# A two-layer diffusion backbone on one core: the third FFN's first product as seven block products for 18 of its 22 pairs, and an earlier place for DeltaNet's gate sums

## Chip, core and metric

The kernel runs on one core of a Trainium2 chip. The metric is the device time of one launch in microseconds (us). Engines are named as the profile names them: PE is TensorE, with PEld its weight loads; DVE is VectorE, ACT ScalarE, POOL GpSimd; SP issues most DMAs. The engines run unsynchronized; each works through its own list of instructions in order and waits on semaphores.

## What is computed

Two layers over 512 tokens, 256 of context and 256 latent, of width 1024. Each layer is a feed-forward network (FFN), a token mixer (DeltaNet in layer 0, windowed attention in layer 1) and a second FFN, each behind a modulated RMS norm. So there are four FFNs; the third, first of layer 1, is the one that the change rewrites. Its mathematics is

```python
def _swiglu(h, w1, w2):
    a, b = jnp.split(h @ w1, 2, axis=-1)
    return (jax.nn.silu(a) * b) @ w2
```

with h 512 x 1024, w1 1024 x 5632 and w2 2816 x 1024, all float32. The modulation vectors (shift, scale, gate) come from the conditioning times a matrix `ada_w` of 1024 x 9216 per layer. DeltaNet's part that the change touches is the running sum of its log gates g over chunks of 64 tokens.

## The kernel before, in words

**Layout.** Activations stand transposed: a tile has 128 channels on the partitions and 512 tokens along the free axis, context in columns 0 to 255 (`CTX`), latent in 256 to 511 (`LAT`). `self.X` is the residual stream (8 tiles), `self.H` the normed input of a product (8 tiles), `self.G` the FFN's gated hidden.

**Products in split form.** A float32 operand is split in two reduced-precision parts (fp32r), `hi` and `lo`, with lo = x - hi; a product is three matmuls: hi·hi, hi·lo, lo·hi (`mm3`, L292). So one 128-wide block of outputs over all 512 tokens and 1024 input channels takes 8 x 3 = 24 matmuls of 128 rows, 128 columns and 512 moving columns.

**An FFN.** The 22 pairs (128 columns of a and the matching 128 of b) go in three parts of 6, 8 and 8 (`self.parts`). For a part, `ffn1_pairs` (L1000) makes each pair with 48 matmuls, in a PSUM tile for a and one for b. `ffn_evac` (L872) is the evacuation: silu(a) on ACT, times b on DVE, copy to `hi` on ACT, subtraction to `lo` on DVE. Then `out_blocks` (L1057) multiplies the part by w2: 8 output tiles, each 3 matmuls for every pair of the part. In the first part of an FFN the first two pairs run the context half first and then the latent half (`halves_first`, L1018), since the normed input arrives by halves and tile by tile (`h_chunks`, L818, fed by ACT, DVE and POOL).

**Weights.** `plan_weights` (L306) lists loads of 1 MB (`raw`, two buffers, and `ub`, two more) and units, the weight blocks in the order of their use. `_split` (L447) makes a unit's `hi` by a copy on ACT and its `lo` by a subtraction on DVE. `w_ahead` (L483) is a background task that keeps up to `LOOK` = 4 units split ahead of the one in use.

**Background work.** `ada_gen` (L682) makes the modulation vectors: for each, 16 steps load a 128x512 piece of `ada_w` and multiply by the conditioning and accumulate, on DVE alone or with the product on ACT and the addition on POOL. In the third FFN it runs until 1371 us.

**What sets the order.** The program's text is written by generators under a planning clock (`Sched`, L69): every matmul advances the clock, and a task runs when the clock reaches the time at which it expects its input (`at`, L249). `spare` (L253) is `at` with 2500 ns more. The clock decides only the place of an instruction in its engine's list; on the chip, semaphores decide the time. The clock holds a cost for each engine's instruction and knows of no interference between engines.

**DeltaNet's gates.** `dn_gates` (L1202) takes the product's gate columns, transposes them on PE, applies softplus and scaling on ACT and DVE, and writes `gs`. Then five small matmuls on `gs` make the sums; from them DVE makes `glb`, `kdl`, `neg` and ACT makes `eg`, `aS`. Around it, `dn_unit` (L1262) takes the keys' tiles through a 5-tap convolution on DVE (four SCALAR_TENSOR_TENSOR after an ACT copy, for each head), silu on ACT, and four transposes on PE.

Of the kernel before, what the change touches and what calls it, by code (L numbers as in the profile page):

```python
# [213 lines left out]
class Kernel:  # L214
# [57 lines left out]
    def mm(self, out, lhsT, rhs, start=True, stop=True, tp=None, ns=None):  # L272
        kw = {} if tp is None else {"tile_position": tp}
# [10 lines left out]
        self.nc.tensor.matmul(out, lhsT, rhs, start=start, stop=stop, **kw)  # L284
        self.s.tick(ns)
# [6 lines left out]
    def mm3(self, ps, w, h, nk, sl=ALL, ks=None, start=True, stop=True):  # L292

        whi, wlo = w
        hhi, hlo = h
        ks = range(nk) if ks is None else ks
        for i, k in enumerate(ks):
            if h is self.H:
                self.h_wait(k, sl)
            wh, wl = whi[k // 4][:, k % 4, :], wlo[k // 4][:, k % 4, :]  # L300
            self.mm(ps[:, sl], wh, hhi[k][:, sl], start=(start and i == 0), stop=False)
            self.mm(ps[:, sl], wh, hlo[k][:, sl], start=False, stop=False)
            self.mm(ps[:, sl], wl, hhi[k][:, sl], start=False, stop=(stop and i == len(ks) - 1))


    def plan_weights(self):  # L306
# [13 lines left out]
        def unit(r, views, shape):  # L320
            for i in r:
                self.raws[i]["left"] += 1
            self.units.append({"r": r, "views": views, "shape": shape, "w": None})

        def cols(mat, r0, nk, c0, w=256):

# [6 lines left out]
        def ffn1(w1, p0, n):  # L333
            if n % 2:
                r = raw((lambda t: t[:, :, 0:128], w1[:, 128 * p0:128 * p0 + 128].rearrange("(k p) c -> p k c", p=128)),
                        (lambda t: t[:, :, 128:256],
                         w1[:, F + 128 * p0:F + 128 * p0 + 128].rearrange("(k p) c -> p k c", p=128)))
                std(r, 0)
                std(r, 1)
                p0, n = p0 + 1, n - 1  # L340
            for p in range(p0, p0 + n, 2):
                ra = cols(w1, 0, 8, 128 * p)
                rb = cols(w1, 0, 8, F + 128 * p)
                for i in range(2):
                    std(ra, i)
                    std(rb, i)

        def rows(w2, p0, n):

# [17 lines left out]
        for l in range(2):  # L367
            for j in range(2):
                w1, w2 = a["ffn_w1"][l, j], a["ffn_w2"][l, j]
                for p0, n in self.parts:  # L370
                    if first:
                        ffn1(w1, 3, 3)
                        first = False
                    else:
                        ffn1(w1, p0, n)
                    (rows if l and j else ffn2)(w2, p0, n)
# [70 lines left out]
    def _split(self):  # L447
        un = self.units[self.u_split]
        nc = self.nc
        tiles = [self.raws[i]["tile"] for i in un["r"]]  # L450
        nk, w = un["shape"]
        hi, lo = [], []
# [28 lines left out]
        self.u_split += 1  # L481

    def w_ahead(self):  # L483

        while self.u_split < len(self.units):
            un = self.units[self.u_split]
            self._load()
            if self.u_split >= self.u_use + self.LOOK or self.urgent and self.u_split > self.u_use and len(self.hready) < 8:
                yield 200
            elif any(i >= self.r_next for i in un["r"]):  # L490
                yield 200
            else:
                t = self.at(*[self.raws[i]["tile"] for i in un["r"]])
                if t:
                    yield t
                else:
                    self._split()
                    yield 100 if self.u_split <= self.u_use + 1 else 1000

    def w_get(self, i=0):  # L500
        while self.u_split <= self.u_use + i:
# [316 lines left out]
    def h_chunks(self, hf, l, slot, ks, pace=None):  # L818
# [16 lines left out]
        for k in ks:  # L835
# [21 lines left out]
    def norm_half(self, hf, sq, l, slot):  # L857
# [7 lines left out]
        if hf == "x":  # L865
            self.tables("silu")
            self.norming = self.urgent = self.lo_mix = False
            if (l, slot) == (0, 2):
                self.ada_pause = self.ada_hold = False


    def ffn_evac(self, pa, pb, sl):  # L872
# [6 lines left out]
        nc.vector.tensor_tensor(out=glo[:, sl], in0=g[:, sl], in1=ghi[:, sl].bitcast(F32), op=ALU.subtract)  # L879
        self.G[0].append(ghi)  # L880
        self.G[1].append(glo)

# [117 lines left out]
    def ffn1_pairs(self, n, sl):  # L1000
        for _ in range(n):
            pa, pb = self.mmt(), self.mmt()
            for ps in (pa, pb):
# [2 lines left out]
                    self.ffn_evac(pa, pb, sl)  # L1006
                self.w_done()

    def mm_narrow(self, ps, w, sl):


# [94 lines left out]
    def ffn(self, l, j, sl, nxt, start=False):  # L1106
        v = 8 if j else 2
        for pi, (p0, n) in enumerate(self.parts):
            self.G = ([], [])
            if pi == 2 and (l, j) == (0, 0):  # L1110
                self.ada_hold = True
            if pi == 0:
# [3 lines left out]
                elif sl is ALL:  # L1116
                    prev = []

                    def evac(i, ps):
                        prev.append(ps)  # L1120
                        if i % 2:
                            self.ffn_evac(prev[i - 1], ps, ALL)

                    self.halves_first(4, evac)
                    self.ffn1_pairs(n - 2, sl)
                else:
                    self.ffn1_pairs(n, sl)
            else:
                self.ffn1_pairs(n, sl)
            last = pi == 2  # L1130
# [71 lines left out]
    def dn_gates(self, ps):  # L1202
# [26 lines left out]
        for e in range(2):  # L1229
            for half in range(2):  # L1230
# [750 lines left out]
    def run(self, upto=None):  # L1981
        self.upto = upto
        nc = self.nc
        self.acc = self.rs = None
        self.table = None
        self.ready = set()
        self.margin = 300.0
# [63 lines left out]
```

## Time and profile before

| | |
|---|---|
| runs | 1920.95 us median of 3 (1920.34 to 1924.17) |
| profiled execution | 1922.17 us, of which the span (first to last instruction) 1920.4 us |
| third FFN in the span | PE dense on its pairs and w2 blocks from 1225 to 1566 us |
| of that, part 1 (8 pairs) | about 1304 to 1392 us |
| of that, part 2 (8 pairs) | about 1435 to 1522 us |
| DeltaNet's gate sums on PE | 435.18 to 436.2 us |

The profile's page gives busy time by engine, the span in slices, the chain that ended last, and the costliest groups. Groups (by form) list instructions of one engine, operation, pair of tile names and shape: count, busy us, mean ns of one, and the idle time before them with what ended it. A timeline merges neighbours of one form: start, length, engine, line, operation, out<-in, count, and in brackets the idle time before and who ended it. Windows give the busy time of every engine in a stretch. Nearly all rows name line 184 or 284, since helpers issue the instructions; groups are told apart by tile names: `mm` is a PSUM tile, `u` an SBUF tile of the general pool, `raw` and `ub` loaded weights, `cc` the conditioning, `mod` a modulation vector, `cw` the convolution's taps.

### The profile page before, as it was taken

How to read it: one execution, taken by the hardware profiler on the slowest of the kernel's cores; microseconds unless marked ns; L12 is line 12 of the kernel's file. 1: busy time of each engine (PE TensorE's matmuls, PEld its weight loads, DVE VectorE, ACT ScalarE, POOL GpSimd, SP SyncE). 2: the span in 40 equal slices, each digit the busy share in tenths (PEclk: the TensorE clock that was granted, in tenths of full speed). 3: DMA queues.
4: the chain of work that ended last, by engine and by line, in shares of the span. 5: the costliest groups of instructions: out<-in, count | busy, mean ns of one | idle time of the engine just before them, and what ended most of it. 6: DMA issues, size and time to landing. Idle time of an engine off the chain costs nothing.

```text
span 1920.4 us, 28976 instructions
## 1 busy us (share of the span) xinstructions
PE 1861.0 (97%) x10719; PEld 1525.2 (79%) x10719; DVE 1286.5 (67%) x2124; ACT 966.7 (50%) x2106; POOL 642.2 (33%) x594
## 2 busy tenths in 40 slices
PE   7999999998999999999999999999999999899998
PEld 5878888897777666798888888888888898688887
DVE  4887877755987965578787885745433345967565
ACT  4544534456466545465444444533332348867553
POOL 3343433353546535354343342321200047330000
PEclk9999999999999998999999999999999999999999
DMA  9655554413322252344555454455323325126561
GB/s 294 217 190 188 172 175 154 129 48 123 94 58 76 67 182 83 127 159 160 192 187 191 159 178 162 138 170 190 129 88 110 110 67 122 55 67 191 193 198 66
DMA packets 238708, 271.70 MB, mean 141 GB/s; under 512 B 12343, under 2 KB 189135, under 8 KB 238567
## 3 DMA queue, kind: packets, MB, share of 16 engines
q1 hardware_dynamic: 237703, 269.15, 43.4%
q8 instruction: 84, 1.38, 0.3%
q10 hardware_dynamic: 720, 0.59, 0.1%
q14 instruction: 57, 0.47, 0.1%
q0 software_dynamic: 144, 0.11, 0.0%
HBM read 259.32 MB, written 10.49 MB: 140 GB/s over the span
## 4 chain that ended last, share of the span: by engine, by line
PE 59%; DVE 9%; ACT 3%; issue 2%; POOL 1%; DMA 0%; DVEq 0%; POOLq 0%; ACTq 0%
PE mm L284 58%; DVE u L184 7%; ACT u L184 3%; DVE big L184 1%; PE mm L289 1%; POOL u L184 1%; DVE st L184 0%; DMA u<-XD 0%; ACT ub L184 0%; DVE ub L184 0%; ACT L184 0%; DVEq L184 0%; ACT sc L184 0%; POOLq L184 0%; ACTq L184 0%
## 5 line engine op out<-in xcount | busy, mean ns | idle before, releaser
L284 PE MATMUL mm<-u 128*128 128x512 f32 (+4 forms) x9480 | 1775.5, 353 | 21.5 <-POOL u L184 9.2
L284 PEld LDWEIGHTS mm<-u 128*128 128x128 f32 (+1 forms) x9480 | 1455.9, 185 | 325.1 <-issue 42.0
L184 POOL TENSOR_TENSOR u<-u 128x512 f32<-128x512 f32 (+4 forms) x386 | 425.6, 1108 | 903.9 <-ACT u L184 863.0
L184 ACT ACTIVATE u<-u 128x256 f32<-128x256 f32 (+8 forms) x361 | 170.9, 485 | 448.7 <-DVE u L184 435.4
L184 ACT ACTIVATE u<-mm 128x128 f32<-128x128 f32 (+5 forms) x382 | 152.0, 414 | 255.9 <-PE mm L284 174.2
L184 DVE TENSOR_TENSOR u<-raw,u 128x512 fp32r<-128x512 f32 (+2 forms) x270 | 220.0, 856 | 56.0 <-ACT u L184 55.9
L184 DVE SCALAR_TENSOR_TENSOR u<-u,cc 128x512 f32<-128x512 f32 x196 | 223.5, 1141 | 8.4 <-DMA u<-in_ada_w 5.2
L184 DVE TENSOR_TENSOR u<-ub,u 128x512 fp32r<-128x512 f32 x252 | 198.7, 831 | 30.7 <-ACT u L184 30.5
L184 ACT ACTIVATE u<-raw 128x512 fp32r<-128x512 f32 (+1 forms) x372 | 206.0, 607 | 8.2 <-PE mm L284 5.2
L184 ACT ACTIVATE u<-u,cc 128x512 f32<-128x512 f32 x224 | 151.8, 712 | 111.8 <-DMA u<-in_ada_w 102.7
L184 POOL TENSOR_TENSOR u<-raw,u 128x512 fp32r<-128x512 f32 x98 | 128.9, 1339 | 146.4 <-ACT u L184 116.5
L184 ACT ACTIVATE u<-ub 128x512 fp32r<-128x512 f32 (+1 forms) x282 | 156.4, 609 | 17.3 <-DVE u L184 8.2
L184 DVE TENSOR_TENSOR u<-u,mm 128x512 f32<-128x512 f32 x66 | 45.3, 686 | 164.1 <-PE mm L284 157.7
L184 DVE TENSOR_TENSOR u<-u 128x512 fp32r<-128x512 f32 (+5 forms) x158 | 98.3, 623 | 66.6 <-ACT u L184 63.3
L184 DVE SCALAR_TENSOR_TENSOR u<-mm,mod,u 128x256 f32<-128x256 f32 x168 | 74.6, 478 | 92.2 <-PE mm L284 91.8
L184 DVE SCALAR_TENSOR_TENSOR u<-u,mod 128x256 f32<-128x256 f32 (+1 forms) x140 | 88.5, 683 | 26.5 <-ACT u L184 26.2
L184 ACT ACTIVATE u<-u,mod 128x256 fp32r<-128x256 f32 (+1 forms) x124 | 56.1, 501 | 52.6 <-DVE u L184 51.8
L184 DVE SCALAR_TENSOR_TENSOR u<-mm,cw,u 128x510 f32<-128x510 f32 (+1 forms) x96 | 71.1, 742 | 11.7 <-ACT u L184 10.0
L289 PE MATMUL mm<-ident,u 128*128 128x128 f32 (+3 forms) x361 | 56.5, 292 | 23.0 <-ACT u L184 12.4
L289 PEld LDWEIGHTS mm<-ident,u 128*128 128x128 f32 (+3 forms) x361 | 43.9, 150 | 35.8 <-ACT u L184 16.4
L184 DVE TENSOR_TENSOR u<-mm,u 128x256 f32<-128x256 f32 (+2 forms) x102 | 41.6, 420 | 36.5 <-ACT u L184 16.2
L184 DVE SCALAR_TENSOR_TENSOR u<-u,aS,mm 128x128 f32<-128x128 f32 x96 | 31.0, 344 | 22.0 <-PE mm L284 21.5
(120 smaller groups left out, 601.5 us busy)
## 6 DMA issues: line engine op xcount, KB each, us to landing
u<-in_ada_w SPq DMA_DIRECT2D x256, 256.0 KB, 5.7
ub<-in_ffn_w SPq DMA_DIRECT2D x60, 1024.0 KB, 5.3
raw<-in_ffn_w SPq DMA_DIRECT2D x58, 1024.0 KB, 5.3
raw<-in_dn_w_in SPq DMA_DIRECT2D x16, 1024.0 KB, 5.7
ub<-in_ada_w SPq DMA_DIRECT2D x12, 512.0 KB, 7.3
ub<-in_ffn_w SPq DMA_DIRECT2D x6, 768.0 KB, 4.8
raw<-in_ffn_w SPq DMA_DIRECT2D x6, 768.0 KB, 5.1
raw<-in_dn_w_out SPq DMA_DIRECT2D x4, 1024.0 KB, 5.6
```

Of the source, the lines that this page charges most:

```text
L184: r = f(*a, **k)
L284: self.nc.tensor.matmul(out, lhsT, rhs, start=start, stop=stop, **kw)
L289: self.nc.tensor.transpose(out, in_, self.ident[:k, :k])
```

## The change

The third FFN's pairs 4 to 21 (18 of 22: all but the first four of part 0) make their first product by a Winograd form of Strassen's scheme. The 1024 x 256 weights of a pair are cut in 2 x 2 blocks (upper and lower 512 input channels; a and b), the input in 2 x 2 blocks (the same channel halves; context and latent). Seven block products replace eight. A block product has 4 x 3 = 12 matmuls of 256 moving columns, so a pair has 84 of them in place of 48 of 512 columns.

- Weights: a pair has seven "forms" in place of two units. POOL makes four sums (S1 = b1 + b2, S2 = S1 - a1, S4 = a2 - S2, S3 = a1 - b1); three forms are the plain blocks a1, a2, b2. Each form has one ACT copy and one DVE subtraction of 128x512 (`_split_form`). A form counts half a unit in `LOOK`, so eight forms may stand ahead.
- Input: `h_forms` makes the four combined input blocks `T` from a full-precision copy `Hf` of the normed input, which `h_chunks` now writes for every tile (before: for odd ones only). The copies of 3 of its 8 split results lie in the `big` pool.
- Evacuation: four partial sums per pair are copied from PSUM by ACT (128x256 each) while PE goes on (`keep`); blocks alternate between the two PSUM tiles of the pair, and a block that adds to a tile waits for the copy of what stood there. `fast_evac` then has two DVE additions from PSUM, silu, product, copy, subtraction.
- `dn_gates` waits with `at` in place of `spare` before the five gate sums.

```diff
+    FAST = {(1, 0)}
+    SLOW = 4
+    FORMS = ("A11", "S1", "S2", "S4", "S3", "A12", "A22")
...
+    def _split_form(self, un, tiles):
...
+        def put(name, x, y, op):
+            st[name] = self.u((128, 4, 128))
+            nc.gpsimd.tensor_tensor(out=st[name], in0=x, in1=y, op=op)
...
+        if f == "A11":
+            put("S1", b1, b2, ALU.add)
+            put("S2", st["S1"], a1, ALU.subtract)
+        elif f == "S1":
+            put("S4", a2, st["S2"], ALU.subtract)
+            put("S3", a1, b1, ALU.subtract)
+        src = {"A11": a1, "A12": a2, "A22": b2}[f] if f[0] == "A" else st[f]
+        hi, lo = self.u((128, 4, 128), F32R), self.u((128, 4, 128), F32R)
+        self.act(out=hi, in_=src, func=AF.Copy)
+        nc.vector.tensor_tensor(out=lo, in0=src, in1=hi.bitcast(F32), op=ALU.subtract)
...
-            if self.u_split >= self.u_use + self.LOOK or self.urgent and self.u_split > self.u_use and len(self.hready) < 8:
+            if self.ahead() >= self.LOOK or self.urgent and self.u_split > self.u_use and len(self.hready) < 8:
...
-            if k % 2:
+            if (l, 0) in self.FAST and slot == 0:
...
+                self.act(out=self.Hf[k][:, sl], in_=t[:, sl], func=AF.Identity, bias=B)
+                f = self.Hf[k] if k % 2 else None
+            elif k % 2:
...
+    def h_forms(self):
...
+        for k in range(4):
+            x, y = self.Hf[k], self.Hf[k + 4]
...
+            sub(nc.vector, t[:, CTX], x[:, LAT], x[:, CTX])
+            sub(nc.vector, t[:, LAT], y[:, LAT], t[:, CTX])
+            sub(nc.gpsimd, v[:, CTX], y[:, LAT], x[:, LAT])
+            sub(nc.vector, v[:, LAT], y[:, CTX], t[:, LAT])
...
+    def fast_pairs(self, n):
...
+            block(pb[:, LAT], H(0, CTX))
+            keep(ta[:, CTX], pb[:, LAT])
+            block(pa[:, LAT], T(0))
+            keep(tb[:, LAT], pa[:, LAT])
+            block(pb[:, LAT], T(1), False)
+            keep(ta[:, LAT], pb[:, LAT])
+            block(pa[:, LAT], H(1, LAT), False)
+            block(pb[:, LAT], T(2), False)
+            keep(tb[:, CTX], pb[:, LAT])
+            block(pa[:, CTX], H(1, CTX), False)
+            block(pb[:, CTX], T(3), False)
...
+    def fast_evac(self, pa, pb, ta, tb):
...
+        nc.vector.tensor_tensor(out=ta, in0=pa, in1=ta, op=ALU.add)
+        yield self.at(ta)
+        self.act(out=ta, in_=ta, func=AF.Silu)
+        nc.vector.tensor_tensor(out=tb, in0=pb, in1=tb, op=ALU.add)
+        yield self.at(ta, tb)
+        nc.vector.tensor_tensor(out=tb, in0=ta, in1=tb, op=ALU.mult)
+        yield self.at(tb)
+        self.act(out=ghi, in_=tb, func=AF.Copy)
+        yield self.at(ghi)
+        nc.vector.tensor_tensor(out=glo, in0=tb, in1=ghi.bitcast(F32), op=ALU.subtract)
...
-        yield self.spare(self.gs)
+        yield self.at(self.gs)
```

**DVE at the gate sums.** The rows stand just behind the writing of `gs` and `lb`; each run of four SCALAR_TENSOR_TENSOR with `cw` is one head's convolution.

```order
 L184 SCALAR_TENSOR_TENSOR u<-mm,cw,u 128x2x255 x2
 L184 SCALAR_TENSOR_TENSOR u<-mm,cw,u 128x2x254 x2
-L184 SCALAR_TENSOR_TENSOR u<-mm,cw,u 128x2x255 x2
-L184 SCALAR_TENSOR_TENSOR u<-mm,cw,u 128x2x254 x2
 L184 TENSOR_TENSOR glb<-mm,lb 128x64
 L184 TENSOR_TENSOR kdl<-mm,glb 128x64
 L184 TENSOR_SCALAR neg<-eg 128x64
+L184 SCALAR_TENSOR_TENSOR u<-mm,cw,u 128x2x255 x2
+L184 SCALAR_TENSOR_TENSOR u<-mm,cw,u 128x2x254 x2
```

One head's convolution moves behind the three small operations on the gate sums.

**PE at the same place, before:**

```order
L284 MATMUL mm<-u 128x256 x63
L284 MATMUL mm<-u 128x512
L284 MATMUL mm<-gs,u 128x32 x2
L284 MATMUL mm<-gs,keep 128x64
L284 MATMUL mm<-gs,u 128x64 x2
L284 MATMUL mm<-u 128x512 x12
L289 MATMUL mm<-ident,u 128x128 x4
```

**and after** (the matmul's line is now 290, the transpose's 295):

```order
L290 MATMUL mm<-u 128x256 x42
L290 MATMUL mm<-gs,u 128x32 x2
L290 MATMUL mm<-gs,keep 128x64
L290 MATMUL mm<-gs,u 128x64 x2
L290 MATMUL mm<-u 128x256 x21
L290 MATMUL mm<-u 128x512 x9
L295 MATMUL mm<-ident,u 128x128 x4
```

The gate sums move ahead of 21 matmuls of 256 columns and one of 512; the keys' first transposes (the last row) move ahead of three more of 512.

**ACT in one pair of part 2, before** (numbers tell the tiles apart): silu, copy to `hi`, and the four copies of two units.

```order
L184 ACTIVATE u_14468<-mm_14400 128x512
L184 ACTIVATE u_14470<-u_14469 128x512
L184 ACTIVATE u_14479<-raw_14220 128x512
L184 ACTIVATE u_14483<-raw_14220 128x512
L184 ACTIVATE u_14513<-raw_14272 128x512
L184 ACTIVATE u_14517<-raw_14272 128x512
```

**and after.** The rows `<-mm` of 128x256 are the four `keep` copies; `u_15491<-u_15463`, `u_15508<-u_15465`, `u_15527<-u_15487`, `u_15543<-u_15489` are the `hi` of S1, S2, S4, S3, whose sources POOL writes; the first row is silu of DVE's sum, `u_15455<-u_15324` the `hi` of DVE's product.

```order
L184 ACTIVATE u_15323<-u_15323 128x512
L184 ACTIVATE u_15459<-mm_15458 128x256
L184 ACTIVATE u_15491<-u_15463 128x512
L184 ACTIVATE u_15460<-mm_15457 128x256
L184 ACTIVATE u_15508<-u_15465 128x512
L184 ACTIVATE u_15455<-u_15324 128x512
L184 ACTIVATE u_15459<-mm_15458 128x256
L184 ACTIVATE u_15527<-u_15487 128x512
L184 ACTIVATE u_15543<-u_15489 128x512
L184 ACTIVATE u_15460<-mm_15458 128x256
L184 ACTIVATE u_15561<-ub_15033 128x512
L184 ACTIVATE u_15576<-ub_15035 128x512
```

Between the copies that PE waits for, ACT's list now holds six instructions that wait for POOL or DVE.

**POOL late in part 1, after.** Rows with `raw` or `ub` are the four weight sums of a pair, `u<-u` are additions of `ada_gen`; before, POOL has only the latter here.

```order
L184 TENSOR_TENSOR u<-raw,u 128x512
L184 TENSOR_TENSOR u<-raw 128x512
L184 TENSOR_TENSOR u<-u 128x512 x3
L184 TENSOR_TENSOR u<-ub 128x512
L184 TENSOR_TENSOR u<-u,ub 128x512
L184 TENSOR_TENSOR u<-ub,u 128x512
L184 TENSOR_TENSOR u<-ub 128x512
L184 TENSOR_TENSOR u<-u 128x512 x3
```

Counted over part 1, ten additions of `ada_gen` on POOL and seven of its multiply-adds on DVE stand among the pairs' own instructions.

More of the change, by code (lines that the diff above doesn't have):

```diff
@@ L269, in tables, with mm @@
             self.nc.scalar.preload_act_table_set({"exp": "natural_log_exp_and_others", "silu": "silu_and_others"}[name])
-    def mm(self, out, lhsT, rhs, start=True, stop=True, tp=None, ns=None):
-        kw = {} if tp is None else {"tile_position": tp}
+    def mm(self, out, lhsT, rhs, start=True, stop=True, tp=None, ns=None, **kw):
+        if tp is not None:
+            kw["tile_position"] = tp
         if ns is None:
@@ L346, in ffn1, with ffn1fast @@
                     std(rb, i)
+        def ffn1fast(w1, p0, n):
+            for p in range(p0, p0 + n, 2):
+                r = [cols(w1, 0, 8, 128 * p), cols(w1, 0, 8, F + 128 * p)]
+                for i in range(2):
+                    st = {"i": i}
+                    for f in self.FORMS:
+                        unit(r, [], (4, 128))
+                        self.units[-1].update(form=f, st=st, size=0.5)
         def rows(w2, p0, n):
@@ L451, in _split @@
         nk, w = un["shape"]
+        if un["form"]:
+            self._split_form(un, tiles)
+            return
         hi, lo = [], []
@@ L481, in _split, with ahead @@
         self.u_split += 1
+    def _split_form(self, un, tiles):
+        nc, st, f = self.nc, un["st"], un["form"]
+        cs = slice(128 * st["i"], 128 * st["i"] + 128)
+        (a1, a2), (b1, b2) = [(t[:, 0:4, cs], t[:, 4:8, cs]) for t in tiles]
+        def put(name, x, y, op):
[11 more added lines that the diff above has]
+        nc.vector.tensor_tensor(out=lo, in0=src, in1=hi.bitcast(F32), op=ALU.subtract)
+        un["w"] = (hi, lo)
+        for i in un["r"]:
+            self.raws[i]["left"] -= 1
+            self.raws[i]["until"] = max(self.s.free[e] for e in ("scalar", "gpsimd", "vector"))
+        self.u_split += 1
+    def ahead(self):
+        return sum(u["size"] for u in self.units[self.u_use:self.u_split])
     def w_ahead(self):
@@ L497, in w_ahead @@
                     self._split()
-                    yield 100 if self.u_split <= self.u_use + 1 else 1000
+                    yield 100 if self.u_split <= self.u_use + 1 else 500 if un["form"] else 1000
     def w_get(self, i=0):
@@ L867, in norm_half @@
             self.norming = self.urgent = self.lo_mix = False
+            if (l, 0) in self.FAST and slot == 0:
+                self.s.add(self.h_forms())
             if (l, slot) == (0, 2):
                 self.ada_pause = self.ada_hold = False
+    def h_forms(self):
+        nc = self.nc
+        for k in range(4):
+            x, y = self.Hf[k], self.Hf[k + 4]
+            t, v = self.u(), self.u()
+            sub = lambda e, o, a, b: e.tensor_tensor(out=o, in0=a, in1=b, op=ALU.subtract)
+            sub(nc.vector, t[:, CTX], x[:, LAT], x[:, CTX])
+            sub(nc.vector, t[:, LAT], y[:, LAT], t[:, CTX])
+            sub(nc.gpsimd, v[:, CTX], y[:, LAT], x[:, LAT])
+            sub(nc.vector, v[:, LAT], y[:, CTX], t[:, LAT])
+            parts = []
+            for i, z in enumerate((t, v)):
+                yield self.at(z)
+                if 2 * k + i < 3:
+                    z2 = self.big(dt=F32R)
+                    hi, lo = z2[:, 0:512], z2[:, 512:1024]
+                else:
+                    hi, lo = self.u(dt=F32R), self.u(dt=F32R)
+                self.act(out=hi, in_=z, func=AF.Copy)
+                yield self.at(hi)
+                sub(nc.gpsimd if i else nc.vector, lo, z, hi.bitcast(F32))
+                parts += [(hi, lo)]
+            self.T.append(parts)
+        self.Hf = {}
     def ffn_evac(self, pa, pb, sl):
@@ L879, in ffn_evac @@
         nc.vector.tensor_tensor(out=glo[:, sl], in0=g[:, sl], in1=ghi[:, sl].bitcast(F32), op=ALU.subtract)
+        self.Gset.add(len(self.G[0]))
         self.G[0].append(ghi)
@@ L1007, in ffn1_pairs, with block, keep @@
                 self.w_done()
+    def fast_pairs(self, n):
+        H = lambda i, sl: [tuple(p[4 * i + k][:, sl] for p in self.H) for k in range(4)]
+        T = lambda i: [tuple(p[:, 256 * (i % 2):256 * (i % 2) + 256] for p in self.T[k][i // 2]) for k in range(4)]
+        nc = self.nc
+        for _ in range(n):
+            pa, pb = self.mmt(), self.mmt()
+            ta, tb = self.u(), self.u()
+            self.s.until(lambda: len(self.T) == 4)
+            def block(out, mov, first=True):
+                kw = {} if first else {"skip_group_check": True}
+                hi, lo = self.w_get()
+                for k in range(4):
+                    hh, hl = mov[k]
+                    self.mm(out, hi[:, k, :], hh, start=(first and k == 0), stop=False, **kw)
+                    self.mm(out, hi[:, k, :], hl, start=False, stop=False, **kw)
+                    self.mm(out, lo[:, k, :], hh, start=False, stop=(k == 3), **kw)
+                self.w_done()
+            def keep(dst, src):
+                self.act(out=dst, in_=src, func=AF.Copy)
+            block(pb[:, LAT], H(0, CTX))
[9 more added lines that the diff above has]
+            block(pb[:, CTX], T(3), False)
+            t = self.fast_evac(pa, pb, ta, tb)
+            next(t)
+            self.s.add(t)
@@ new lines, in fast_evac @@
+    def fast_evac(self, pa, pb, ta, tb):
+        nc = self.nc
+        slot, done = len(self.G[0]), self.Gset
+        ghi, glo = self.u(dt=F32R), self.u(dt=F32R)
+        self.G[0].append(ghi)
+        self.G[1].append(glo)
+        yield 0
+        nc.vector.tensor_tensor(out=ta, in0=pa, in1=ta, op=ALU.add)
[8 more added lines that the diff above has]
+        nc.vector.tensor_tensor(out=glo, in0=tb, in1=ghi.bitcast(F32), op=ALU.subtract)
+        done.add(slot)
@@ L1108, in ffn @@
         for pi, (p0, n) in enumerate(self.parts):
-            self.G = ([], [])
+            self.G, self.Gset = ([], []), set()
+            slow = 6 if (l, j) not in self.FAST else self.SLOW
             if pi == 2 and (l, j) == (0, 0):
@@ L1122, in evac @@
                             self.ffn_evac(prev[i - 1], ps, ALL)
+                    self.T = []
                     self.halves_first(4, evac)
-                    self.ffn1_pairs(n - 2, sl)
+                    self.ffn1_pairs(slow - 2, sl)
+                    self.fast_pairs(n - slow)
                 else:
                     self.ffn1_pairs(n, sl)
+            elif (l, j) in self.FAST:
+                self.fast_pairs(n)
             else:
```

13 lines of the change are left out of this document (11 added, 2 removed).

## The prediction

> **What bounds the kernel now.** I read the page's busy shares first, then the chain of work that ended last between 1190 and 1600 us (start, length, what), then PE's timeline of the same stretch.
>
> ```profile
> span 1920.4 us, 28976 instructions
> PE 1861.0 (97%) x10719; PEld 1525.2 (79%) x10719; DVE 1286.5 (67%) x2124; ACT 966.7 (50%) x2106; POOL 642.2 (33%) x594
> 1278.67 51.31 PE mm L284 x224
> 1330.37 51.31 PE mm L284 x224
> 1382.06 185.62 PE mm L284 x868
> 1330.30 46.54 PE L284 MATMUL mm<-u 128*128 128x512 f32 x204
> 1567.32 13.78 PE L284 MATMUL mm<-u 128*128 128x256 f32 x112
> ```
>
> PE is busy 97% of the span, and in the third FFN the chain names nothing but PE: every wait of the others is hidden, with POOL at a third and DVE at two thirds. So work taken from PE there shows in the time one for one, as long as the others keep their cover. A matmul of 512 columns follows the one before after (46.54 - .39) / 203 = .2273 us (.39 being the last one's pass through the array), one of 256 columns after (13.78 - .28) / 111 = .1216. Half the width costs 53.5% of the time.
>
> **PE's gain.** A pair took 48 x .2273 = 10.91 us and will take 84 x .1216 = 10.21, so 18 pairs save 18 x .70 = 12.6; I write **-12.5**. The scheme's seven eighths would be 1.36 a pair; half of that goes to the dearer narrow matmul. Were narrow ones to cost exactly half, 18 x 1.36 = -24.5 would come out; the 112 in a row speak against it.
>
> **What a pair now asks of the others.** ACT, DVE and POOL groups by form: ACT and the first two DVE rows from part 2, 1440 to 1520 us, where POOL rests (the 128x256 row is of the whole span), the rest from 1280 to 1380, where `ada_gen` runs.
>
> ```profile
> L184 ACT ACTIVATE u<-ub 128x512 fp32r<-128x512 f32 x14 | 7.8, 616 | 0.0
> L184 ACT ACTIVATE u<-mm 128x512 f32<-128x512 f32 x7 | 4.2, 598 | 38.1 <-PE mm L284 38.1
> L184 ACT ACTIVATE u<-mm 128x256 f32<-128x256 f32 x56 | 21.1, 380 | 49.4 <-PE mm L284 48.4
> L184 DVE TENSOR_TENSOR u<-ub,u 128x512 fp32r<-128x512 f32 x16 | 10.1, 685 | 0.0
> L184 DVE TENSOR_TENSOR u<-u,mm 128x512 f32<-128x512 f32 x6 | 4.1, 688 | 40.0 <-PE mm L284 40.0
> L184 DVE TENSOR_TENSOR u<-raw,u 128x512 fp32r<-128x512 f32 x17 | 15.7, 961 | 0.0
> L184 DVE SCALAR_TENSOR_TENSOR u<-u,cc 128x512 f32<-128x512 f32 x14 | 10.5, 749 | 0.2
> L184 POOL TENSOR_TENSOR u<-u 128x512 f32<-128x512 f32 x14 | 20.0, 1429 | 83.4 <-ACT u L184 83.0
> ```
>
> ACT goes from four copies, a silu and a copy (5 x .62 + .60 = 3.7 us) to eight copies, silu and four keeps: 8 x .62 + .60 + 4 x .38 = 7.1 of 10.21, so it still fits by sum. DVE goes from six operations to eleven, 6 to 7 us undisturbed. POOL gets four, which fit too if each engine were by itself. They aren't: the same DVE subtraction takes .685 with POOL at rest and .961 in the mean beside it. The two timelines side by side show it piece by piece.
>
> ```profile
> 1303.76 3.48 DVE L184 TENSOR_TENSOR u<-raw,u 128x512 fp32r<-128x512 f32 x2
> 1358.54 1.29 DVE L184 TENSOR_TENSOR u<-raw,u 128x512 fp32r<-128x512 f32 x2
> 1303.68 1.29 POOL L184 TENSOR_TENSOR u<-u 128x512 f32<-128x512 f32 x1 [4.39 <-ACT u L184]
> 1305.34 1.34 POOL L184 TENSOR_TENSOR u<-u 128x512 f32<-128x512 f32 x1 [0.36 <-ACT u L184]
> ```
>
> Two subtractions alone take 1.29 us (.685, then the next .60 later); between two additions of POOL they take 3.48, that is 1.74 each. One took POOL's turn and its own: 1.74 - .60 = 1.14 for POOL. So I count POOL's and DVE's two-operand work from SBUF as one queue, 1.14 and .60 an item. A pair asks of it four sums and, of DVE, seven `lo`, the product and its `lo`: 4 x 1.14 + 9 x .60 = **9.96 us against PE's 10.21**; if the two additions with an operand in PSUM queue as well, 11.16. The Trainium skill, "SBUF — State Buffer", section "Who interferes with whom", says that a DVE instruction with two SBUF inputs and a GpSimd instruction that reads SBUF exclude one another for a whole instruction, and that one with at most one SBUF input does not contend. The 1.74 beside .60 agrees; by it a pair is at 9.96, and it speaks against the change, since the new sums stand on the one engine that shares with the busiest helper.
>
> Lag then reaches PE through ACT: its four keeps a pair, which PE waits for two blocks later (slack one block, 12 x .1216 = 1.46, less the keep's .38 and hand-over, about .9), are queued in order behind copies that wait for POOL's S1, S2, S4, S3 and behind silu and the `hi` copy that wait for DVE. The forms ahead (LOOK: eight) are the only other cover.
>
> **Part 1, +7.** Eight pairs ask 8 x 9.96 = 79.7 us; `ada_gen`'s seven multiply-adds by .75 (taken at their length, none is two-operand for sure) and ten additions by 1.14 add 16.6: 96.3. Of it the first pair's forms, 4 x 1.14 + 7 x .60 = 8.8, can be done before the part begins, leaving 87.5 against PE's 8 x 10.21 = 81.7: at least 5.8 late. With no reach ahead, 7 x 9.96 + 16.6 - 7 x 10.21 = 14.8. I take 7, near the low end, as SP's loads come in time for a reach ahead today.
>
> **Part 0, +2.** Before the first fast pair the queue gets, by the same prices, eight slow splits and eight operations of evacuation (9.6), about five of each `ada_gen` operation (9.5), `h_forms` (per k three DVE halves at .3, a `lo` at .60, POOL's half at .57 and `lo` at 1.14: 12.9) and the first forms (8.8): 41, against three slow pairs, 33, of PE. So 0 to 8; 2, since the first pairs' halves leave DVE slack. **Part 2, +2.** There `ada_gen` is over; at 9.96 nothing is late, at 11.16 it is 7 x .95 = 6.7.
>
> **The norm, +0.8.** Rows of ACT, POOL and PE before the FFN's first matmuls.
>
> ```profile
> 1217.57 2.77 ACT L184 ACTIVATE u<-u,mod 128x256 fp32r<-128x256 f32 x6 [1.39 <-DVE u L184]
> 1222.58 0.72 POOL L184 TENSOR_TENSOR u<-u 128x256 fp32r<-128x256 f32 x1 [1.30 <-ACT u L184]
> 1223.35 1.09 PE L284 MATMUL mm<-u 128*128 128x256 f32 x7 [0.73 <-POOL u L184]
> ```
>
> PE waits here for ACT's chain by way of POOL. Four more full-precision writes in the latent half cost 2.77 / 6 = .46 each, 1.8 if all delay it, 0 if all fall in ACT's waits (1.39 above); the four of the context half lie beside PE's older work.
>
> **DeltaNet's gates, -4.** PE, DVE, ACT, and last the window 445 to 450 (length, busy PE, PEld, DVE, ACT, POOL, granted clock).
>
> ```profile
> 435.18 0.53 PE L284 MATMUL mm<-gs,u 128*128 128x32 f32 x4
> 436.21 3.01 PE L284 MATMUL mm<-u 128*128 128x512 f32 x12
> 444.71 1.21 PE L289 MATMUL mm<-ident,u 128*128 128x128 f32 x4 [5.49 <-ACT u L184]
> 445.57 5.04 PE L284 MATMUL mm<-u 128*128 128x512 f32 x11
> 450.88 1.40 PE L284 MATMUL mm<-u 128*128 128x512 f32 x5
> 433.40 1.29 DVE L184 SCALAR_TENSOR_TENSOR gs<-u,ea 64x32 f32<-64x32 f32 x1
> 435.95 6.10 DVE L184 SCALAR_TENSOR_TENSOR u<-mm,cw,u 128x510 f32<-128x510 f32 x8
> 441.97 0.21 DVE L184 TENSOR_TENSOR glb<-mm,lb 128x64 f32<-128x64 f32 x1
> 444.24 0.72 ACT L184 ACTIVATE u<-u 128x256 f32<-128x256 f32 x2
> 445.00:450.00 5.00, 5.00 (x15) 4.02 (x15) 0.96 (x2) 2.35 (x11) 0.00 (x0) 0.50 0.00 0
> ```
>
> PE stands 5.49 us for the silu at 444.24. The first head's convolution is done by 439.0 (half of 6.10), but ahead of its silu ACT has `eg` and `aS` ahead of it, which wait for `kdl` and `glb`, and these for both convolutions at 435.95. With one of them (3.05) behind, `glb` comes at 438.9, silu at 441.2, the transposes at 441.7. PE pays for it: it reaches the sums 21 x .1216 + .23 = 2.8 earlier, at 432.4, while the last `gs` is written at 434.69 (433.40 + 1.29): a stand of 2.3. From there five small ones (1.0) and 2.6 + 9 x .2273 bring it to about 440.3, so 1.4 idle in place of 5.49. At 441.7 it is 3.0 earlier than before, with four 512s less behind it (.9): 2.1 net. Besides, after the 5.49 stand eleven matmuls take 5.04 us, twice the .2273, at a granted clock of .50; if no long stand precedes, 11 x .23 = 2.5 more is saved: 4.6. I take 4; the bounds are -5 and +1 (the stand of 2.3 costs, the other stays, since seven 512s more now stand ahead of the last decay combinations, 1.6). The step issues no DMA; on POOL the products on `gs` pass two `lo` subtractions, on SP nothing moves for it. The Trainium skill, "TensorE: Matmul & The Clock Gate", section "What's actually happening", says that one idle window of about 3.4 us brings PE down to half clock. The 5.49 with .50 behind agrees; by it both new stands are short enough, and by a finer rule they would not be, which is R3's case.
>
> **SP.** A weight load is now freed in the order of forms, two loads of a couple of pairs at a time, and `ada_gen`'s fetches stand behind them in its queue. The page has 5.3 to 5.7 us from issue to landing against 20 a couple; I count nothing.
>
> **Sum.** -12.5 + .8 + 2 + 7 + 2 - 4 = **-4.7**. The profiled execution, 1922.17 (span 1920.4 and 1.8 around it), becomes 1917.5. The median of the runs shown is 1.2 lower, 1920.95, so I forecast **1916.2**.
>
> **The rivals.**
> - R1, the cover holds: no lag in any part, -12.5 + .8 - 4 = -15.7, so 1905.2 (1909 with nothing from the gates). For it: DVE's third of idle time, eight forms ahead. Against: 9.96 of 10.21 leaves no room for `ada_gen`. Chance .15.
> - R2, slower: the shared queue becomes the bound. At 11.16 a pair with `ada_gen` in full, part 0 is 8 late, part 1 7 x 11.16 + 16.6 - 7 x 10.21 = 23.2, part 2 6.7: 37.9 in all. Half-way between my 11 and this, 24.4, gives -15.7 + 24.4 = +8.7, 1929.6; the full price 1943. It decides from 15.7 + 3.8 = 19.5 of lag, 1.08 a pair, barely more than the keep's slack. For it: POOL's 1.429 mean beside DVE, and three engines chained in order. Against: part 2 has no `ada_gen`. Its rule is that of "SBUF — State Buffer" in the Trainium skill. Chance .25.
> - R3, the gates give nothing (their order moves, the stand only changes place, or the clock falls all the same), the rest as forecast: -.7, 1920.2. Chance .15.
>
> **How the numbers follow.** The forecast has .45. A measurement of this kernel can tell about 0.2%, 3.8 us, from no change: faster means under 1917.1, slower over 1924.8. Of the forecast's .45, .33 falls below and .12 within; R1's .15 is faster, R3's within, R2's slower: faster .48, same .27, slower .25. The range takes the forecast with its lags' bounds (5.8 and 29.5 at the ends, most of it between 5 and 18: 1910 to 1923), R1's nearer half and R2 to its half-way price: 1907 to 1931, leaving out about .1 at each end. The likeliest case's own range is 1910 to 1923.
>
> **What would show it.** A row of 256-column matmuls in the fast pairs spaced .1216, 10.21 a pair, shows the gain. Lag shows as idle PE before them, released by ACT from `mm` or `u`, more in part 1 (PE's eight pairs about 88 to 89 us) than in part 2 (84); DVE's two-operand mean above 1 us in both shows the queue. If part 2 is as late as part 1, `ada_gen` wasn't the cause; if neither is late, R1 holds. At the gates: a stand of about 2.3 near 432, one of 1.4 before transposes near 441.7, and a clock near 1.00 from 440 on. The forecast fails if the fast matmuls aren't spaced .1216, or if DVE and POOL don't queue as in those rows.

## The result and the profile after

The changed kernel takes 1935.01 us (median of 4 runs, 1934.29 to 1938.17) where the kernel before took 1920.64 beside it (1918.38 to 1924.17): 14.4 us more, a ratio of 1.0076 with a 95% interval of 1.0057 to 1.0095. The forecast was 1916.2 with a range of 1907 to 1931, so the time lies outside, on the side of the rival R2.

The page of the profile after, its span and busy shares, and the chain of waits between 1280 and 1540 us by line:

```profile
span 1933.1 us, 30715 instructions
PE 1861.6 (96%) x11367; PEld 1555.1 (80%) x11367; DVE 1412.4 (73%) x2230; ACT 1027.2 (53%) x2248; POOL 770.7 (40%) x674
by line: PE mm L290 48.7%; DVE u L184 29.1%; issue 9.4%; POOL u L184 6.3%; ACT u L184 6.0%; PE mm L295 0.2%; DVE mod L184 0.1%; ACTq L184 0.1%; DVEq L184 0.1%; POOLq L184 0.0%
```

PE's busy time hasn't fallen, though the fast pairs need less of it; and the chain, which named nothing but PE in this stretch before, now runs through DVE, POOL and ACT for 41% of it.

Where the time goes is read from landmarks. DVE's rows `u<-mm,mod,u` of 128x256 take the blocks of w2 out of PSUM, 168 in either trace; the first of a part marks the end of its pairs. The table has the length of each stage before, and what each execution differs by (us; e1 to e4 are the first experiments below, named so throughout):

```
stage                        before    after  e1_gates  e2_ffn  e3_sums_dve  e4_part2
start to 109                 108.8     +2.0     +0.2     +1.6      +0.7        +1.2
401 to 795, DeltaNet         394.3    -10.3     -7.7     -7.1      -6.7        -6.8
norm ahead of third FFN       45.2     +0.5      0.0     +0.5      +0.5        +0.5
part 0, pairs                 73.7     +9.6      0.0     +9.6     +11.1        +0.5
part 0, w2 blocks             29.0      0.0      0.0      0.0      +1.1         0.0
part 1, pairs                 95.8     +9.9      0.0     +9.9      -5.9         0.0
part 2, pairs                 92.1     -1.5      0.0     -1.8      -6.4        -1.7
behind the third FFN         338.4     +2.6     +0.9     -1.2       0.0        +1.4
```

Stages that aren't listed differ by .4 at most. The third FFN's rows repeat to .3 us between after and e2, so they can be trusted from one execution; start, DeltaNet and the stage behind are less steady. Counted as the prediction does (a pair .70 cheaper on PE), the lag is 9.6 + 1.4 = 11.0 in part 0, 9.9 + 5.6 = 15.5 in part 1 and -1.5 + 5.6 = 4.1 in part 2: **30.6 us in place of my 11**.

PE, ACT and DVE near the end of part 1, where PE stands longest (timelines; in brackets the idle time before a row and who ended it):

```profile
1388.59 0.88 PE L290 MATMUL mm<-u 128*128 128x256 f32 x6
1393.00 2.93 PE L290 MATMUL mm<-u 128*128 128x256 f32 x12 [3.53 <-ACT u L184]
1386.63 0.38 ACT L184 ACTIVATE u<-mm 128x256 f32<-128x256 f32 x1 [1.05 <-PE mm L290]
1391.53 1.15 ACT L184 ACTIVATE u<-u 128x512 f32<-128x512 f32 x2 [4.51 <-DVE u L184]
1392.58 0.36 ACT L184 ACTIVATE u<-mm 128x256 f32<-128x256 f32 x1
1387.44 3.45 DVE L184 TENSOR_TENSOR u<-ub,u 128x512 fp32r<-128x512 f32 x2
1390.82 0.68 DVE L184 TENSOR_TENSOR u<-mm,u 128x512 f32<-128x512 f32 x1
1393.00:1399.00 6.00, 6.00 (x29) 6.00 (x30) 4.83 (x6) 2.99 (x7) 2.38 (x2) 0.52 0.00 0
```

Read from DVE's rows. DVE spends 3.45 us on two subtractions beside POOL, so its addition for silu comes at 1390.82. ACT waits 4.51 for it with silu (the first of its two at 1391.53), and the keep copy that PE needs, ready since about 1389.5, stands behind silu until 1392.58. PE waits 3.53 and then works for some 6 us at a granted clock of .52 (last row, a window): 29 matmuls where 6.0 / .1216 = 49 would go, 2.5 us more. Part 0 has such a pair too, stands of 3.72 and 2.38 and then a clock of .50:

```profile
1253.64 0.80 PE L290 MATMUL mm<-u 128*128 128x256 f32 x2 [3.72 <-DVE u L184]
1256.82 1.65 PE L290 MATMUL mm<-big,u 128*128 128x256 f32 x6 [2.38 <-ACT u L184]
1256.00:1262.00 6.00, 5.18 (x24) 5.18 (x25) 6.00 (x5) 4.34 (x9) 5.90 (x4) 0.50 0.06 23
```

That is 5.18 - 24 x .1216 = 2.3 us more by the clock.

The three longest stands of part 2 (1473.61, 1484.60 and 1524.60 us), and those at 1340.84, 1367.27 and 1377.26 in part 1, look alike in the trace: ACT waits 1.6 to 5.8 us for DVE, with silu or with the product's copy, the keep copy runs right behind it, and then PE goes on.

### The profile page after: what moved, and what is told of

The parts are those of the page before. It is cut to its first block, busy times and chain, and to the rows that moved or that the text cites. A ratio compares the mean times of both kernels' runs of the same rounds, so it can differ in the third digit from the quotient of the medians.

```text
span 1933.1 us, 30715 instructions
## 1 busy us (share of the span) xinstructions
PE 1861.6 (96%) x11367; PEld 1555.1 (80%) x11367; DVE 1412.4 (73%) x2230; ACT 1027.2 (53%) x2248; POOL 770.7 (40%) x674
## 4 chain that ended last, share of the span: by engine, by line
PE 74%; DVE 14%; ACT 6%; issue 4%; POOL 2%; DMA 1%; DVEq 0%; ACTq 0%; POOLq 0%
PE mm L290 73%; DVE u L184 12%; ACT u L184 5%; POOL u L184 2%; PE mm L295 2%; DVE big L184 1%; DMA u<-in_ada_b 0%; DVE st L184 0%; DMA u<-XD 0%; ACT L184 0%; ACT ub L184 0%; DVE ub L184 0%; DVE gs L184 0%; DVE lb L184 0%; ACT big L184 0%
## 5 line engine op out<-in xcount | busy, mean ns | idle before, releaser
L290 PE MATMUL mm<-u 128*128 128x512 f32 (+6 forms) x9804 | 1741.3, 343 | 29.8 <-ACT u L184 10.5
L290 PEld LDWEIGHTS mm<-u 128*128 128x128 f32 (+2 forms) x9804 | 1449.3, 186 | 301.1 <-issue 41.4
L184 POOL TENSOR_TENSOR u<-u 128x512 f32<-128x512 f32 (+4 forms) x393 | 437.9, 1121 | 679.9 <-ACT u L184 636.1
L184 ACT ACTIVATE u<-u 128x512 fp32r<-128x512 f32 (+7 forms) x456 | 228.3, 514 | 424.9 <-DVE u L184 397.1
L184 ACT ACTIVATE u<-mm 128x128 f32<-128x128 f32 (+4 forms) x436 | 168.7, 400 | 243.3 <-PE mm L290 164.4
L184 DVE TENSOR_TENSOR u<-u 128x512 fp32r<-128x512 f32 (+5 forms) x262 | 210.5, 822 | 64.1 <-ACT u L184 59.9
L184 POOL TENSOR_TENSOR u<-raw,u 128x512 fp32r<-128x512 f32 (+1 forms) x106 | 141.8, 1360 | 146.5 <-ACT u L184 105.0
L184 DVE TENSOR_TENSOR u<-mm,u 128x256 f32<-128x256 f32 (+2 forms) x138 | 66.0, 487 | 35.9 <-PE mm L290 16.2
L184 DVE TENSOR_TENSOR u<-u,mm 128x512 f32<-128x512 f32 x48 | 32.8, 684 | 49.3 <-PE mm L290 48.3
L290 PE MATMUL mm<-big,u 128*128 128x256 f32 x324 | 53.5, 293 | 11.0 <-ACT u L184 10.8
```

Source lines behind the costliest of these rows:

```text
L184: r = f(*a, **k)
```

## Experiments: each edit alone, sums on DVE, part 2 alone

e1 is the kernel before with

```diff
-        yield self.spare(self.gs)
+        yield self.at(self.gs)
```

> The kernel before with only the gate sums moved. Between the landmarks at 401 and 795 us the changed kernel gained 10.3 us on before, of which 6.3 by 464 us. Theory: the move of the gate sums makes all of it, 1920.6 - 10.3 = 1910.3. Rival: it makes only the local 6.3 (1914.3), and the rest is that execution's clock further on. Second rival: the FFN's edits shift the plan there too, and the move alone gives under 4 (over 1916.6).

Measured 1915.51 beside 1920.50, ratio .9979 (.9967 to .9992): 5.0 us by the medians (4.0 by the ratio), interval 1.5 to 6.3. e2 is the changed kernel with that line undone:

> The changed kernel with the gate sums back at their old place, so the seven-block FFN alone. If the two edits are independent, the FFN costs the third FFN's 18.5 us plus about 1.6 behind it: 1940 to 1945, and 6.3 to 10.3 more than the changed kernel's 1935.0. If the gate move gave nothing of its own: 1935.

Measured 1938.62, ratio 1.0106 (1.0082 to 1.0131), 18.1 over before by the medians (20.4 by the ratio; its four runs spread from 1933.58 to 1944.09). Within that spread the two edits add up: -5.0 + 18.1 = 13.1 against 14.4. The table shows that my 10.3 for the gates was too much: DeltaNet's stretch is 7.1 shorter than in the first trace in e2 too, where nothing moved. Only the start of `glb` after the landmark at 401 separates cleanly: 3.04 to 3.08 earlier in the four kernels with the move, 0.00 in e2; PE's first matmul with `maskr`, at 463.6 before, is 6.3 earlier in all four and 1.4 in e2. PE in the changed kernel:

```profile
435.02 0.41 PE L290 MATMUL mm<-gs,u 128*128 128x32 f32 x2 [0.49 <-DVE gs L184]
436.67 0.41 PE L290 MATMUL mm<-gs,u 128*128 128x32 f32 x2 [1.24 <-DVE gs L184]
443.61 0.85 PE L295 MATMUL mm<-ident,u 128*128 128x128 f32 x4 [1.22 <-ACT u L184]
445.00:450.00 5.00, 5.00 (x25) 4.08 (x24) 3.01 (x6) 4.24 (x20) 0.00 (x0) 1.00 0.19 68
```

Two short stands, .49 + 1.24 and 1.22, stand for the 5.49, and the clock stays at 1.00.

e3 puts a pair's four weight sums on DVE:

```diff
-            nc.gpsimd.tensor_tensor(out=st[name], in0=x, in1=y, op=op)
+            nc.vector.tensor_tensor(out=st[name], in0=x, in1=y, op=op)
```

> The changed kernel with a pair's four weight sums on DVE in place of POOL. Queue theory (POOL and DVE's two-operand work take turns, POOL's turn being the dear one, 1.14 to 1.74): a pair's queue falls from 9.96 or more to 13 x .60 = 7.8 us against PE's 10.21, so part 2 loses its 4.1 of lag, part 1 (additions of the modulation stay) nearly all of its 15.5, part 0 half of its 11: about 25 less, 1910. Order theory (PE waits because its keep copies stand on ACT behind instructions that wait for DVE, and DVE's list is what is long): DVE has four more operations a pair, so the lag stays or grows: 1935 to 1950.

Measured 1916.73, ratio .9982 (.9973 to .9992). DVE has four operations more a pair, and parts 1 and 2 lose all their lag: -5.9 and -6.4. In part 0 the lag stays (11.1, and 1.1 behind it), which the queue theory had not said, so the total misses its 1910 by 6.7. e4 makes seven-block pairs in part 2 alone (in the plan of weights and in `ffn`):

```diff
-                        m = 0 if p0 else self.SLOW
+                        m = 0 if p0 == 14 else n
```

> The changed kernel with seven-block pairs in part 2 alone (8 pairs); parts 0 and 1 as before. If the modulation's background work (over by 1371 us) is what makes parts 0 and 1 late, these lose 9.6 + 9.9 of cost, part 2 keeps its own -1.5 or reaches its -5.6: 1935.0 - 19.5 - (0 to 4) = 1911 to 1915.5. If a pair overfills the queue by itself, part 2 stays at -1.5 or worse, 1915 to 1917; if it lives on forms made ahead in the changed kernel only, part 2 gets longer than before: over 1919.

Measured 1915.68, ratio .9976 (.9965 to .9987). Part 2 stays at -1.7: its lag is its own, neither carried over nor the modulation's, which is over by then. Making the input forms in part 0 without using them there costs .5.

## Experiments: what in POOL's sums costs time

e6 and e7 take e3 and add, beside each sum on DVE, an instruction on POOL that writes a tile nobody reads:

```diff
+            dead = self.u((128, 4, 128))
+            nc.gpsimd.tensor_tensor(out=dead, in0=x, in1=y, op=op)
```

in e6, and `nc.gpsimd.memset(dead, 0.0)` in e7.

> Weight sums on DVE, and the same four sums made a second time on POOL, into a tile that nobody reads; the result is complete. Nobody waits for POOL's sums here, so only what they take from DVE can show. Exclusion theory: a pair asks 13 x .60 + 4 x 1.14 = 12.4 us of the shared queue against PE's 10.21: 2.2 a pair, 17 a part, so parts 1 and 2 go from 5.9 and 6.4 less than before to about 11 more each; total 1916.7 + 25 to 40 = 1942 to 1957. Chain theory (the lag of the changed kernel came from ACT and DVE waiting for the value of a sum that POOL made late): no change, 1916 to 1919.

> As the run with the dead sums, but POOL writes zeros of the same size, four times a pair, and reads nothing; nobody reads them. If POOL's reading is what DVE's two-operand work excludes: no change from 1916.7 (1915 to 1919), and DVE's subtraction keeps its quiet .68. If any POOL instruction on 128x512 excludes it: as the dead sums, over 1930.

Measured: dead sums 1972.57, ratio 1.0271 (1.0256 to 1.0286); zeros 1918.53, ratio .9989 (.9975 to 1.0002). With dead sums part 1 goes from 5.9 less than before to 23.9 more and part 2 from 6.4 less to 11.6 more, some 30 and 18 us. In part 2, with the clock at 1.00 and no compute engine waiting for POOL or a DMA, the 18 are near the 17 that the exclusion theory gave. Part 1's 30, and with them the total above the 1942 to 1957 expected, hold more than that: ACT waits there for POOL's dead sums too (once for 3.57 us, at 1390.40), PE's stands of 2.8 to 4.1 us bring the granted clock down to .91 in the mean, and the modulation runs beside it. With zeros part 1 is 4.7 less than before in place of 5.9, and part 2 the same 6.4 less. DVE's groups by form from 1440 to 1540 us show how, first e3, then dead sums, then zeros with POOL's own group behind it:

```profile
L184 DVE TENSOR_TENSOR u<-raw,u 128x512 fp32r<-128x512 f32 x19 | 12.5, 687 | 4.3 <-ACT u L184 4.3
L184 DVE TENSOR_TENSOR u<-mm,u 128x512 f32<-128x512 f32 x16 | 11.0, 685 | 0.0
```

```profile
L184 DVE TENSOR_TENSOR u<-raw,u 128x512 fp32r<-128x512 f32 x10 | 11.1, 1121 | 0.0
L184 DVE TENSOR_TENSOR u<-mm,u 128x512 f32<-128x512 f32 x9 | 6.1, 679 | 0.0
L184 POOL TENSOR_TENSOR u<-raw,u 128x512 f32<-128x512 f32 x4 | 7.0, 1738 | 0.0
```

```profile
L184 DVE TENSOR_TENSOR u<-raw,u 128x512 fp32r<-128x512 f32 x19 | 12.4, 686 | 4.2 <-ACT u L184 4.2
L184 POOL MEMSET u<- 128x512 f32 x28 | 14.4, 529 | 66.3 <-PE mm L290 45.7 <-DVE u L184 20.5
```

The subtraction from two SBUF tiles goes from 687 to 1121 ns beside POOL's additions; the addition with one operand in PSUM stays at 679; beside POOL's zeros the subtraction keeps its 686. So what costs DVE's tensor_tensor time is POOL's reading, and only where DVE reads two tiles from SBUF. The Trainium skill, "SBUF — State Buffer", section "Who interferes with whom", says that a DVE instruction with two SBUF inputs contends with a GpSimd instruction that reads SBUF and not with one that only writes, and that one with at most one SBUF input doesn't contend outside the modes that use two ports. The trace agrees in these three cases. The exception, which the prediction left out when it gave the rule, may show as well: the modulation's TENSOR_SCALAR, with one tile from SBUF, takes .48 us alone and .95 or 1.59 beside an addition of POOL (the changed kernel at 1220.25, e9 at 1334.46); which mode it ran in no trace shows.

## Experiments: part 0, and ACT's order

e5 is e3 with part 0 as before, so 16 fast pairs:

```diff
-                        m = 0 if p0 else self.SLOW
+                        m = 0 if p0 else n
```

> Weight sums on DVE, and seven-block pairs in parts 1 and 2 alone (16 pairs); part 0 as before, so its input forms have all of part 0 to be made. With the sums on DVE in the earlier run, parts 1 and 2 took 5.9 and 6.4 us less than before and part 0 11.1 + 1.1 more. If part 0's cost is that its fast pairs need forms that DVE hasn't finished, it goes: 1916.7 - 12 = 1904.5. Rival: part 0's cost is the making of the input forms itself, wherever they are used: 1914 to 1917.

Measured 1907.26, ratio .9933 (.9916 to .9950): part 0 at +.6, part 1 -3.4, part 2 -6.4; that part 1 keeps only 3.4 of e3's 5.9 is why the total is over the 1904.5 expected. So the loss of part 0 is in its fast pairs' waiting, not in the making of the forms. e8 holds the modulation's work back until part 0's pairs are through, with the sums on DVE:

```diff
+            while self.ada_stop:
+                yield 500
             while self.ada_pause and (h, k) == (0, 0):
...
+                    self.ada_stop = (l, j) in self.FAST
                     self.halves_first(4, evac)
                     self.ffn1_pairs(slow - 2, sl)
                     self.fast_pairs(n - slow)
+                    self.ada_stop = False
```

> Weight sums on DVE, and the modulation's background work held back during part 0's pairs (eight multiply-adds on DVE and as many products on ACT and additions on POOL move behind it). If part 0 is late because DVE has more to do than PE's time there (sum theory), its 11.1 falls by the 8 x .66 to 8 x .75 taken from DVE and POOL's share, to 2 to 5, and parts 1 and 2 lose at most 3: 1908 to 1911. If it is late because of the order of the chain from the normed input over the forms to the keep copies, part 0 keeps 9 to 11: 1915 to 1917.

Measured 1908.35, ratio .9939 (.9925 to .9954). Part 0 goes from +11.1 to -3.9; some of it is the modulation's own matmuls, which now stand in later stages (+1.8 in part 0's w2 blocks, part 1 -2.7, part 2 -4.6). The three parts with their w2 blocks come to -3.9 + 1.8 - 2.7 - 4.6 = -9.4, where e3 had 11.1 + 1.1 - 5.9 - 6.4 = -.1. So the modulation's work made part 0 late. Its multiply-adds on DVE, its additions on POOL and its products on ACT move together here, so that DVE's load alone did it, as the sum theory says, fits but isn't shown. DVE's groups of the changed kernel from 1217 to 1254 us, where the first fast pair waits, and the window's sum:

```profile
L184 DVE SCALAR_TENSOR_TENSOR u<-u,cc 128x512 f32<-128x512 f32 x7 | 7.3, 1038 | 0.0
1217.00:1254.00 37.00, 33.28 (x190) 29.11 (x189) 33.71 (x43) 16.49 (x31) 18.29 (x13) 0.97 0.32 107
```

DVE is busy for 33.7 of 37.0 us, and 7.3 of that is the modulation, for which nobody waits yet.

e9 is the changed kernel, sums on POOL, with two waits of the evacuation planned 2500 ns later:

```diff
-        yield self.at(ta)
+        yield self.spare(ta)
         self.act(out=ta, in_=ta, func=AF.Silu)
...
-        yield self.at(tb)
+        yield self.spare(tb)
         self.act(out=ghi, in_=tb, func=AF.Copy)
```

> The changed kernel (weight sums on POOL) with silu and the copy of the product planned 2500 ns later each, so that on ACT fewer instructions that wait for DVE stand ahead of the keep copies; the work of each engine is the same. The runs with the sums on DVE and with dead sums showed the queue of POOL and DVE; open is whether it reaches PE by ACT's order. Order theory: the keeps run on time, PE's stands in parts 1 and 2 (12.4 and 4.1 in the changed kernel) fall by half or more, 1935.0 - 8 = 1927. Sum theory (whoever waits, the queue is 1 to 6 us a part too long): the stands move to another wait, 1932 to 1937.

Measured 1921.55, ratio 1.0011 (1.0001 to 1.0022): 13.5 less than the changed kernel (12.5 by the two ratios), more than I had expected even of the order theory. Part 0 is unchanged at +10.3, part 1 goes from +9.9 to +1.3, part 2 from -1.5 to -6.4. The windows of part 2, the changed kernel and then e9 (length, busy PE, PEld, DVE, ACT, POOL, clock):

```profile
1456.00:1548.00 92.00, 88.90 (x702) 86.34 (x702) 76.24 (x93) 50.18 (x104) 37.22 (x24) 1.00 0.38 123
```

```profile
1452.00:1545.00 93.00, 93.00 (x714) 90.24 (x713) 76.29 (x96) 51.81 (x107) 34.46 (x22) 1.00 0.39 125
```

DVE and POOL are nearly as busy and as much in each other's way as before (DVE's subtractions `u<-u` take 1025 ns in the mean, before 1024), and in part 2 PE no longer stands. The edit moves two lists: on ACT silu goes behind the next pair's first two keeps, and on DVE the pair's second addition goes behind three subtractions of forms. That ACT's list is the one that counts rests on the stands shown above, each ended by a keep behind silu or the product's copy; no run moved ACT's list alone. The longest stand left in part 1 is 1.49 by the spacing of matmuls, where it was 3.69, and the window from 1312 to 1415 has a clock of 1.00 where the changed kernel's had .95.

## Experiments: a better version

> Weight sums on DVE, the modulation's work held back in part 0's pairs and, in the whole third FFN, made on DVE alone (one multiply-add in place of ACT's product and POOL's addition), so POOL's 128x512 work is out of the fast parts. Held back with POOL's additions, the parts came to -3.9 + 1.8, -2.7 and -4.6 against before. Exclusion theory: without POOL's additions the two later parts come near the -5.9 and -6.4 of the run without holding: 1908.4 - 4 = 1904. Sum theory on DVE: ten more multiply-adds at .66 a part on DVE take back what the additions gave: 1908.

> Weight sums on DVE, seven-block pairs in parts 1 and 2, and the modulation on DVE alone in the third FFN. With POOL's additions part 1 came to -3.4 against before, part 2 to -6.4, total 1907.3. Exclusion theory: part 1 gains up to 2.5: 1905 to 1906. If part 1's 2.5 is its first pair's forms (w2's blocks of part 0 hold DVE), nothing: 1907.

e10 is e8, e11 is e5, both with the modulation made on DVE alone in the third FFN (`in_fast` is true there):

```diff
-                if (conds.index(cd) if len(conds) == 2 else h):
+                if not self.in_fast and (conds.index(cd) if len(conds) == 2 else h):
```

Measured: e10 1905.30, ratio .9930 (.9906 to .9953), part 1 -4.0 and part 2 -4.6; e11 **1904.59**, ratio .9928 (.9910 to .9946), part 1 -4.7 in place of -3.4. Both beat the kernel before and the changed one; they can't be told apart, and from e5 and e8 only by 2.7 and 3.1 us with intervals that overlap; of e11's gain 1.3 is seen in part 1. Against e8, e10 gains 1.3 in part 1 and nothing in part 2, less than the exclusion theory had said.

e12 is e10 with the later silu of e9:

> All edits that helped, on all 18 pairs: weight sums on DVE, the modulation held back in part 0's pairs and on DVE alone in the third FFN, silu and the product's copy planned 2500 ns later. The run without the later silu had stands of 1.4 and .6 us left in the three parts. If ACT's order makes these, they go: 1905.3 - 2 = 1903. If they are DVE's own load: 1905.

Measured 1912.09, ratio .9953 (.9937 to .9969): worse than e10 by 6.8, or 4.4 by the two ratios, and not the 1903 to 1905 expected. PE now stands behind the pairs, at the w2 blocks, which need the last pair's product:

```profile
1391.29 0.96 PE L290 MATMUL mm<-u 128*128 128x512 f32 x3 [0.59 <-DVE u L184]
1394.41 1.65 PE L290 MATMUL mm<-u 128*128 128x512 f32 x3 [2.16 <-DVE u L184]
1396.46 3.78 PE L290 MATMUL mm<-u 128*128 128x512 f32 x8 [0.40 <-DVE u L184]
```

The eight matmuls of the last row take 3.78 us where 8 x .2273 is 1.8: the clock is .52 from 1394 to 1400. Where DVE is on time, a later silu makes the last pair late; that it paid in e9 because DVE was late there is my reading of the two runs. That a shorter delay, or one for all but a part's last pair, would serve both wasn't tried.

## Why the prediction was wrong

- **PE's gain** was right in its kind and a little small. In the changed kernel 21 matmuls of 256 columns take 2.68 us, (2.68 - .28) / 20 = .120 each, not .1216. Where nobody is late, a part of eight pairs is 6.4 shorter (e3, e9), not 5.6.

```profile
1380.59 2.68 PE L290 MATMUL mm<-u 128*128 128x256 f32 x21
```

- **The queue of DVE and POOL** was the right mechanism, at about the right price: dead sums lengthened part 2 by 18 us where the price gives 17 (e6). The additions with a PSUM operand don't queue (.680 beside POOL), so 9.96 a pair was the value and 11.16 wasn't. Part 1's own overrun was forecast as 7 and is 1.3 + 5.6 = 6.9 when ACT's order doesn't add to it (e9), or 7.7 with the gain of 6.4. The 7 was picked from 5.8 to 14.8, so that it came this close is partly luck. Part 2's is nothing, as 9.96 against 10.21 says.
- **The step that failed is the one from the queue to PE.** The prediction saw that the keeps stand on ACT behind silu, the product's copy and the forms' copies, and then took as lag only what the queue's sum exceeds PE's. With .9 us of slack, longer delays of an addition or a product on DVE passed to PE through silu or the product's copy, whether or not the sum fitted. (PE waits for three of a pair's four keeps, not all: no block adds to a tile behind the last.) That made part 2's 4.1 (all gone in e9) and 8.6 of part 1's 15.5, the clock's share included: 12.7 us together, of which the sum had only part 2's 2. Part 2 loses its lag by either remedy, sums on DVE (e3) or a later silu (e9), so it takes both, the delay beside POOL and the order behind it.
- **Part 0, +2 of 0 to 8**, should have been at the upper end. The 41 us of work against 33 already gave the 8; "the first pairs' halves leave DVE slack" was wrong, as DVE was busy for nine tenths of the time, the modulation's work among it. Lag there was 11.0, with the clock's 2.3 in it, and holding the modulation back removed it (e8, with the sums on DVE).
- **The clock** was weighed at the gates alone. PE's stands of 3.5 us and more in parts 0 and 1 were followed by .50 and .52, some 2.3 + 2.5 us that no term had. A third, of 3.29 at 1340.84, was followed by .72 from 1340 to 1346: 31 matmuls in 5.16 us of busy PE, some 1.4 more.
- **The gates, -4**: 5.0 by the medians of e1, 1.5 to 6.3 by its interval. `glb` 3.06 earlier (3.05 forecast), stands of 1.7 and 1.2 (2.3 and 1.4), the clock at 1.00.
- **The norm, +.8**: .5.
- **The rivals.** R2 came true by its condition, a lag over 19.5: 30.6 less 15.7 is 14.9, and 14.4 was measured. But its mechanism was half of it: I priced it by a dearer pair (11.16), and the rest came from ACT's order, part 0 and the clock. It had .25 and should have had more, since every term of lag was taken near its low end.

What stays open is DeltaNet's stretch, which differs by up to 6 us between executions of kernels that issue it alike; no run here was made for it. The granted clock differs there too, .97 in the first trace and .98 in the changed kernel's (401 to 790 us), but the runs don't line up by it.

## What to carry to other kernels

Before giving PE's saved time away to helpers, add up each stage's two-operand work of DVE and reading work of POOL as one queue, with the background work that runs there; a sum on the busier engine can be cheaper than on the idle one. Then look at every short copy on which PE waits: what stands ahead of it on its engine, and what that waits for, sets PE's stands even where the sums fit. A stand of about 3 us or more may cost the slow clock behind it as well: in e6 stands of 2.93 and 3.19 us (at 1392.98 and 1328.76) were followed by 3 us or more at .50, but one of 2.88 (at 1414.72), and one of 3.08 in e1 (at 517.22), by a clock of 1.00.

## What the runs showed of the hardware

That POOL's additions slow DVE was known from the trace before; that they do so for results nobody reads, by 18 us in part 2 and some 30 in part 1 with what follows from it, and that zeros of the same size (529 ns each on POOL) leave DVE's subtraction at 686 ns and part 2 as it was, was not.
